# Zero rows for the low key parts of a differential attention, and another order of the first loads

## The chip, the cores and the metric

One core of a Trainium2 chip runs the whole program. The metric is the device time of one execution in microseconds (us). TensorE (PE in the rows, PEld for its weight loads) does the matmuls, VectorE (DVE) and ScalarE (ACT) the elementwise work, GpSimd (POOL) some small work, and SyncE (SP) issues most DMAs. The input and the weights lie in HBM and are read once.

## The reference

Two decoder layers over 256 tokens of width 1024, and a last norm. Of a layer, cut to what matters:

```python
h = _rms_norm(x, attn_norm)
proj = h @ w_in                       # q, k, v of A and B, latents of C, three gates
y_a = _diff_attention(aq, ak, av, lam, lam_init, slopes_a, diff_norm) @ w_branch_a
y_b = _dilated_attention(bq, bk, bv, slopes_b) @ w_branch_b
y_c = _mla(c_q, c_kv_pe, q_norm, w_uq, kv_norm, w_ukv, pos) @ w_branch_c
x = x + (g_a * y_a + g_b * y_b + g_c * y_c) @ w_out
h2 = _rms_norm(x, ffn_norm)
x = x + (silu(h2 @ w_ffn_gate) * (h2 @ w_ffn_up)) @ w_ffn_down

# in _diff_attention: 4 heads, each with 2 components c of 64 dimensions
s = einsum('bqhcd,bkhcd->bhcqk', q, k) * scale - slopes * dist     # causal
p = softmax(s); p = p[:, :, 0] - lam * p[:, :, 1]
```

## The kernel before

**Precision.** Every matmul works on pairs of fp32r tiles: a high part (ScalarE's copy that rounds, `hi_of`, L223) and the low part that is left (VectorE's difference, `lo_of`, L228 and L230). A product is the sum of three: high by high, high by low, low by high.

**Weights.** All weights are packed in the order of use into pieces of at most 128 x 1024 (`PLAN`). A piece is read into one of five `raw` buffers (`dma_piece`, L242, on SP's queue), split into one of five `whi` and `wlo` buffers (`split_piece`) and taken by TensorE (`take`). `split_piece` asks for the next DMA. The first eight pieces of a layer (128 x 672) make the latents of branch C, the next eight (128 x 1024) its differential queries and keys.

**Work in two streams.** `dense(l)` is a generator that yields after every piece; `run` and `attention` pull it by `pump(n)` between the small stages of attention (scores, softmax terms, transposes, values). The order of each engine's instructions then comes from a scheduler that reorders this program; its result is fixed when the program is built.

**The first 25 us.** `setup` issues, on SP: x transposed (`x0`, four tiles of f, 256 KB each, the first one in two halves), five weight pieces between them, then x once more in rows (`x_tm`, two tiles of 512 KB). `first_norm` splits `x0` into pairs and pumps one piece of the latent projection for each of its four tiles; then `squares` sums the squares of `x_tm` (L392), `norm_factors` makes the row factors r (L399, GpSimd's power in L373), `norm_diag` puts them on a diagonal (high and low half, L411 and L230) and `norm_rows` spreads them over all rows by two matmuls with ones (`ones_r`). The latents stay in two banks and two att buffers of PSUM until `latent_scaled` copies them out times r (L651, L654); `latent_transposed` transposes them (L692). The query and key tiles are copied out times the spread row factors (L513, L515).

**The stacked scores.** A head of branch A has two components of 64 dimensions, so one 128-row tile holds both. `stacked` makes for a query tile, per component c, a tile with the high part in the 64 rows of c and the low part in the other 64; for a key tile, per c, a tile with the high part in both halves, and one tile `low` that has the low parts of both components, each in its own 64 rows. One matmul of 128 rows then gives high by high plus low by high, and the third product needs 64 rows. `stacked_scores` (four heads, two components, two query blocks) issues

```python
self.mm(ps[:, 0:256], q[:, 128:256], kk, True, False)          # 128 rows
self.mm(ps[:, 0:256], q[rows, 128:256], low, False, True)      # rows: the 64 of c
```

and the same for the first query block with 128 columns, so a layer has 32 such matmuls, 16 of them with 64 rows.

**Room.** `fr` is a ring of 17 tiles of 128 x 1024, given out by halves or whole; `pt` a ring of 6 for the transposed probabilities; `row` one of 2 for the spread row factors.

Of the kernel before, what the change touches and what calls it, by code (L numbers as in the profile page):

```python
# [12 lines left out]
F32 = mybir.dt.float32  # L13
F32R = mybir.dt.float32r
# [17 lines left out]
SL = (slice(256, 384), slice(0, 256))  # L32
MASKED = 3.0e32
PIECE = 1024
N_PAIR = 17
N_F = 9
N_DENSE = 4
N_RAW = 5
# [145 lines left out]
class Build:  # L184
    def __init__(self, nc, tc, ctx, x, xt, w, gains, lam, fnorm, cst, out):
        self.nc, self.tc = nc, tc
        self.x_in, self.xt_in, self.w_in, self.gains_in = x, xt, w, gains
        self.lam_in, self.fnorm_in, self.cst_in, self.out = lam, fnorm, cst, out
        self.cp = cp = ctx.enter_context(tc.tile_pool(name="cp", bufs=1))
        pp = ctx.enter_context(tc.tile_pool(name="pp", bufs=1, space=PSUM))  # L190

        def ring(n, cols, dt, name, pool=cp):
            return Ring([pool.tile([128, cols], dt, name=f"{name}{i}") for i in range(n)])

        self.banks = ring(N_DENSE, 512, F32, "bank", pp)
        self.att = ring(8 - N_DENSE, 512, F32, "att", pp)
        self.fr = PairRing([cp.tile([128, 1024], F32R, name=f"fr{i}") for i in range(N_PAIR)])
        self.f = ring(N_F, 512, F32, "f")
        self.s = ring(5, 384, F32, "s")
        self.pt = ring(6, 384, F32R, "pt")  # L200
        self.small_tiles = ring(32, 4, F32, "small")
        self.row = ring(2, 256, F32, "row")
        self.raw = [cp.tile([128, PIECE], F32, name=f"raw{i}") for i in range(N_RAW)]
        self.whi = [cp.tile([128, PIECE], F32R, name=f"whi{i}") for i in range(N_PIECE)]
        self.wlo = [cp.tile([128, PIECE], F32R, name=f"wlo{i}") for i in range(N_PIECE)]
        self.taken = self.n_split = self.n_dma = self.woff = 0
# [82 lines left out]
    def setup(self):  # L289
        nc, cp = self.nc, self.cp  # L290
        self.gains = cp.tile([128, G_W], F32, name="gains")
        nc.scalar.dma_start(out=self.gains, in_=self.gains_in)
        self.x0 = [self.f.get() for _ in range(4)]
        x0 = [split_rows(t) for t in self.x0]
        self.x_tm = [cp.tile([128, D], F32, name=f"x_tm{b}") for b in range(2)]
        for p in range(4):
            if p == 0:
                nc.sync.dma_start(out=x0[0][:, 0], in_=self.x_in[:, 0, :])
                self.dma_piece()
                nc.sync.dma_start(out=x0[0][:, 1], in_=self.x_in[:, 1, :])  # L300
            else:
                nc.sync.dma_start(out=x0[p], in_=self.x_in[:, 2 * p:2 * p + 2, :])  # L302
                self.dma_piece()
        for _ in range(N_RAW - 4):
            self.dma_piece()
        for b in range(2):
            nc.sync.dma_start(out=self.x_tm[b], in_=self.xt_in[b])
        self.ones = cp.tile([128, 128], F32, name="ones")
        nc.vector.memset(self.ones, 1.0)
        self.ones_r = cp.tile([128, 128], F32R, name="ones_r")  # L310
        nc.vector.tensor_copy(self.ones_r, self.ones)
        warm = self.small()
        nc.scalar.activation(out=warm, in_=self.ones[:, 0:2], func=AF.Exp)
        bank = self.banks.get()
        for _ in range(WARM):
            self.mm(bank[:, 0:128], self.ones, self.ones, True, True)
        self.banks.put(bank)
        self.mhalf = cp.tile([128, 2], F32, name="mhalf")
        nc.gpsimd.memset(self.mhalf, -0.5)
        self.ident = cp.tile([128, 128], F32, name="ident")  # L320
        nc.sync.dma_start(out=self.ident, in_=self.cst_in[:, C_ID:C_ID + 128])
        self.vc = [cp.tile([128, 8, 2, 64], F32R, name=f"vc{b}") for b in range(2)]
        self.q_tm = cp.tile([128, 2, 8, 96], F32, name="q_tm")
        self.k_tm = cp.tile([128, 2, 8, 96], F32, name="k_tm")
        self.kpe = cp.tile([128, 2, 32], F32, name="kpe")

    def tables(self):
# [97 lines left out]
    def first_norm(self, pump):  # L425
        self.fresh_norm()
        for p in range(4):
            self.split_pair(p, split_rows(self.x0[p]), G_ATT)
            if p < AHEAD:
                self.split_piece()  # L430
            pump(1)
        self.f.put(*self.x0)
        self.ss = [self.small(), self.small()]
        for n in range(2):
            self.squares(n)
        self.norm_factors()
# [49 lines left out]
        self.split(*fields(kd[rows]), src)  # L486
        return kd

    def stacked(self, t, query):
        halves = (slice(0, 64), slice(64, 128))  # L490
        out = [self.fr.get() for _ in range(2)]
        for c in range(2):
            self.hi_of(out[c][halves[c]], t[halves[c]])
        if query:
            for c in range(2):
                self.lo_of(out[c][halves[1 - c]], t[halves[c]], out[c][halves[c]])
            return out
        low = self.fr.get()
        for c in range(2):
            self.hi_of(out[c][halves[1 - c]], t[halves[c]])  # L500
            self.lo_of(low[halves[c]], t[halves[c]], out[c][halves[c]])
        return out + [low]

    def qk_proj(self, q, k, scale, stacked):
        nc = self.nc
        for j in range(4):
# [8 lines left out]
                nc.vector.tensor_tensor(out=tv, in0=ps, in1=self.Rb, op=ALU.mult)  # L515
            self.banks.put(bank)
            if stacked:
                (q if j < 2 else k).append(self.stacked(t, j < 2))
            elif j < 2:
                hi, lo = self.fr.get(), self.fr.get()  # L520
                self.split(hi, lo, t)
                q.append((hi, lo))
            else:
                k.append(self.key_pair(tv))
# [212 lines left out]
    def stacked_scores(self, h, c):  # L737
        ps = self.att.get()
        cs = slice((h % 2) * 256, (h % 2) * 256 + 256)
        rows = slice(c * 64, c * 64 + 64)  # L740
        q, kk, low = self.qa[h // 2][c][:, cs], self.ka[h // 2][c][:, cs], self.ka[h // 2][2][rows, cs]
        self.mm(ps[:, 0:256], q[:, 128:256], kk, True, False)
        self.mm(ps[:, 0:256], q[rows, 128:256], low, False, True)
        self.mm(ps[:, 256:384], q[:, 0:128], kk[:, 0:128], False, False)
        self.mm(ps[:, 256:384], q[rows, 0:128], low[:, 0:128], False, True)
        return self.softmax_terms(ps, self.ta[h])

    def softmax_terms(self, ps, table, parts=False):
# [313 lines left out]
    def run(self):  # L1062
        self.n_norm = 0
        self.setup()
        for l in range(DEPTH):
            stream = self.dense(l)

            def pump(n):
                for _ in range(n):
                    next(stream)  # L1070
# [5 lines left out]
            else:  # L1076
                self.first_norm(pump)
            self.norm_diag()
            pump(2)
            self.norm_rows()  # L1080
            pump(2)
            self.latent_scaled()
            if l == 0:
                self.tables()
# [5 lines left out]
            pump(1)  # L1090
            self.latent_transposed(l, 2)
            self.latent_factors(l)
            pump(5)
            pump(5)
            pump(4)
            self.attention(l, pump)
            for _ in stream:
                pass
# [53 lines left out]
```

## Time and profile before

| | |
|---|---|
| median of 3 runs | 894.67 us (894.23 to 896.05) |
| profiled execution | 896.65 us, its span 894.8 us |
| TensorE, VectorE, ScalarE, GpSimd busy | 886.5, 591.9, 504.5, 66.4 us |
| mean granted TensorE clock | 0.997 |
| read from HBM | 154.03 MB, 173 GB/s over the span |

The span runs from the first to the last instruction, so 1.85 us of the profiled execution lie outside it. The execution that was profiled is 1.98 us longer than the median of the timed runs. A busy engine has an instruction in it; since matmuls overlap, the time that one of them costs is the distance from its start to the next one's start.

### The profile page before, as it was taken

The page shows a single profiled execution, that of the slowest core. Times are in us where ns is not written, and L with a number is a line of the kernel's source. Part 1 is how long each engine was busy: PE and PEld are TensorE (multiplying, and loading weights), DVE is VectorE, ACT ScalarE, POOL GpSimd, SP SyncE. Part 2 cuts the span into 40 slices and gives each one's busy share as a digit, 9 for nine tenths or more (in the row PEclk, how much of TensorE's full clock was granted, in tenths as well). Part 3 has the DMA queues.
Part 4 walks back from the last instruction along what each step waited for, and adds up shares of the span by engine and source line. Part 5 has one row for each costly group of instructions (what it writes and reads, how often), then busy time and mean ns, then how long its engine had stood idle before and what let it go on. Part 6 is the DMA issues. An engine that isn't in the chain of part 4 may idle for free.

```text
span 894.8 us, 12732 instructions
## 1 busy us (share of the span) xinstructions
PE 886.5 (99%) x4710; PEld 763.9 (85%) x4710; DVE 591.9 (66%) x990; ACT 504.5 (56%) x852; POOL 66.4 (7%) x91
## 2 busy tenths in 40 slices
PE   9999999999999999999999999999999999999997
PEld 8988988888888888888899799888888888888886
DVE  6967978756665666555467778787655666556444
ACT  7875766654554444444376767766444554444332
POOL 1830220000000000000011303000000000000000
PEclk9999999999999999999999999999999999999999
DMA  9745344456556666666465454444565566655541
GB/s 336 256 145 188 119 142 145 139 170 196 180 172 196 189 188 183 183 179 191 142 210 176 139 169 138 142 144 161 166 203 173 165 203 197 193 187 185 188 142 48
DMA packets 45423, 155.92 MB, mean 174 GB/s; under 512 B 5168, under 2 KB 6192, under 8 KB 45360
## 3 DMA queue, kind: packets, MB, share of 16 engines
q1 hardware_dynamic: 44928, 154.55, 54.4%
q8 instruction: 37, 0.61, 0.3%
q10 hardware_dynamic: 432, 0.55, 0.2%
q14 instruction: 26, 0.21, 0.1%
HBM read 154.03 MB, written 1.05 MB: 173 GB/s over the span
## 4 chain that ended last, share of the span: by engine, by line
PE 97%; DMA 1%; issue 1%; SPq 0%; ACT 0%; DVE 0%; POOLq 0%; POOL 0%
PE bank L210 85%; PE att L210 7%; PE att L443 2%; DMA x_tm<-xt 1%; PE att L718 1%; PE att L767 0%; PE att L769 0%; PE att L768 0%; ACT f L392 0%; SPq L242 0%; PE att L692 0%; PE att L851 0%; DVE x_tm L1043 0%; SPq L302 0%; ACT x_tm L1058 0%
## 5 line engine op out<-in xcount | busy, mean ns | idle before, releaser
L210 PE MATMUL bank<-whi,fr 128*128 128x512 f32 (+1 forms) x2032 | 632.6, 387 | 1.1 <-ACT whi L223 1.1
L228 DVE TENSOR_TENSOR wlo<-raw,whi 128x1024 fp32r<-128x1024 f32 (+2 forms) x294 | 353.3, 1203 | 250.3 <-ACT whi L223 249.1
L223 ACT ACTIVATE whi<-raw 128x1024 fp32r<-128x1024 f32 (+2 forms) x294 | 305.0, 1040 | 309.8 <-PE bank L210 255.3
L210 PEld LDWEIGHTS bank<-whi,fr 128*128 128x128 f32 x2032 | 380.4, 188 | 73.9 <-ACT whi L223 1.6
L210 PE MATMUL bank<-wlo,fr 128*128 128x512 f32 (+1 forms) x1016 | 390.6, 386 | 0.0
L210 PEld LDWEIGHTS bank<-wlo,fr 128*128 128x128 f32 x1016 | 191.3, 188 | 36.3 <-DVE wlo L228 0.9
L210 PE MATMUL bank<-fr,whi 128*128 128x256 f32 x512 | 95.3, 285 | 0.0
L210 PEld LDWEIGHTS bank<-fr,whi 128*128 128x128 f32 x512 | 80.1, 191 | 0.2
L210 PE MATMUL bank<-fr,wlo 128*128 128x256 f32 x256 | 73.0, 285 | 0.0
L210 PEld LDWEIGHTS bank<-fr,wlo 128*128 128x128 f32 x256 | 49.0, 191 | 0.0
L373 POOL TENSOR_TENSOR r<-small,mhalf 128x2 f32<-128x2 f32 x4 | 2.8, 706 | 480.0 <-DVE small L399 480.0
L759 ACT ACTIVATE s<-s,small 128x256 f32<-128x256 f32 (+1 forms) x80 | 35.7, 450 | 3.5 <-DVE small L757 3.2
L210 PE MATMUL att<-fr,fr 96*128 96x256 f32 (+5 forms) x184 | 36.5, 301 | 0.0
L210 PEld LDWEIGHTS att<-fr,fr 96*128 96x128 f32 (+2 forms) x184 | 28.3, 188 | 7.0 <-issue 1.4
L223 ACT ACTIVATE fr<-att 128x512 fp32r<-128x512 f32 (+2 forms) x54 | 28.4, 558 | 6.7 <-PE att L210 4.0
L373 POOL TENSOR_TENSOR small<-small,mhalf 128x2 f32<-128x2 f32 (+1 forms) x12 | 10.1, 844 | 294.1 <-DVE small L1047 178.5
L210 PE MATMUL att<-whi,fr 128*128 128x288 f32 (+1 forms) x108 | 29.8, 289 | 0.0
L228 DVE TENSOR_TENSOR fr<-att,fr 128x512 fp32r<-128x512 f32 (+2 forms) x46 | 28.2, 636 | 0.9 <-ACT fr L223 0.6
L223 ACT ACTIVATE fr<-f 64x512 fp32r<-64x512 f32 (+2 forms) x40 | 23.3, 582 | 5.0 <-DVE f L513 2.7
L972 ACT ACTIVATE f<-bank,rh 128x512 f32<-128x512 f32 (+1 forms) x24 | 15.6, 654 | 12.2 <-PE bank L210 12.2
L614 ACT ACTIVATE f<-bank,rh 128x512 f32<-128x512 f32 x24 | 16.3, 689 | 8.7 <-PE bank L210 8.5
L228 DVE TENSOR_TENSOR fr<-f,fr 64x512 fp32r<-64x512 f32 (+2 forms) x32 | 20.2, 631 | 0.4
(130 smaller groups left out, 615.4 us busy)
## 6 DMA issues: line engine op xcount, KB each, us to landing
raw<-w SPq DMA_DIRECT2D x272, 512.0 KB, 3.6
raw<-w SPq DMA_DIRECT2D x16, 336.0 KB, 3.1
raw<-w SPq DMA_DIRECT2D x6, 384.0 KB, 3.6
x_tm<-xt SPq DMA_DIRECT2D x2, 512.0 KB, 8.0
f<-x SPq DMA_DIRECT2D x3, 256.0 KB, 5.3
f<-fnorm SPq DMA_DIRECT2D x2, 256.0 KB, 4.2
out<-x_tm ACTq DMA_DIRECT2D x2, 256.0 KB, 2.2
f<-x SPq DMA_DIRECT2D x2, 128.0 KB, 2.9
```

The costliest lines, as they stand in the source:

```text
L210: self.nc.tensor.matmul(out, lhsT, rhs, start=start, stop=stop, skip_group_check=True)
L223: self.nc.scalar.activation(out=hi, in_=src, func=AF.Copy, scale=scale)
L228: self.nc.vector.tensor_tensor(out=lo, in0=src, in1=h, op=ALU.subtract)
L373: self.nc.gpsimd.tensor_tensor(out=out, in0=v, in1=self.mhalf[:, 0:v.shape[1]], op=ALU.pow)
L443: self.nc.tensor.transpose(ps[:, c, b * 128:b * 128 + 128], src[b][:, c0 + c * 128:c0 + c * 128 + 128], self.ident)
L614: nc.scalar.activation(out=t[b], in_=bank[b], func=AF.Tanh, scale=self.rh[:, b:b + 1])
L718: nc.tensor.transpose(ps[0:96, c, b * 128:b * 128 + 128], src[:, b, 2 * p + c, :], self.ident)
L759: nc.scalar.activation(out=s[:, SL[b]], in_=s[:, SL[b]], func=AF.Exp, bias=mn[:, b:b + 1], scale=-1.0, accum_out=z[:, b:b + 1])
L972: nc.scalar.activation(out=a, in_=g, func=AF.Tanh, scale=self.rh[:, b:b + 1])
```

## The change

- The low parts of the differential keys move from halves of the `fr` ring into four tiles of their own (`low`, one per key tile and component). Each has the low part of component c in the 64 rows of c and zeros in the other 64, which GpSimd writes once in `setup`. The matmul with the low part then takes all 128 rows of the query tile; its number and its columns stay the same.
- To make room, `fr` has 16 tiles (the low parts leave it), `pt` 5 and `row` 1.
- On SP the second weight piece is asked for ahead of the second tile of x, and so on, one piece before each tile; `x_tm` is no longer issued in `setup` but after the third and the fourth `pump` of `first_norm`.
- In layer 0 five pieces more are pumped ahead of the squares, and the pumps behind `norm_diag` and `norm_rows` and one later one fall away: 25 in all, as before. In layer 1 the numbers stay.

```diff
-N_PAIR = 17
+N_PAIR = 16
...
-        self.pt = ring(6, 384, F32R, "pt")
+        self.pt = ring(5, 384, F32R, "pt")
...
-        self.row = ring(2, 256, F32, "row")
+        self.row = ring(1, 256, F32, "row")
...
-        for p in range(4):
-            if p == 0:
-                nc.sync.dma_start(out=x0[0][:, 0], in_=self.x_in[:, 0, :])
-                self.dma_piece()
-                nc.sync.dma_start(out=x0[0][:, 1], in_=self.x_in[:, 1, :])
-            else:
-                nc.sync.dma_start(out=x0[p], in_=self.x_in[:, 2 * p:2 * p + 2, :])
-                self.dma_piece()
-        for _ in range(N_RAW - 4):
+        nc.sync.dma_start(out=x0[0][:, 0], in_=self.x_in[:, 0, :])
+        self.dma_piece()
+        nc.sync.dma_start(out=x0[0][:, 1], in_=self.x_in[:, 1, :])
+        self.dma_piece()
+        for p in range(1, 4):
+            nc.sync.dma_start(out=x0[p], in_=self.x_in[:, 2 * p:2 * p + 2, :])
             self.dma_piece()
-        for b in range(2):
-            nc.sync.dma_start(out=self.x_tm[b], in_=self.xt_in[b])
...
+        self.low = [[cp.tile([128, 512], F32R, name=f"low{j}_{c}") for c in range(2)] for j in range(2)]
+        for low in self.low:
+            for c in range(2):
+                nc.gpsimd.memset(low[c][64 - c * 64:128 - c * 64].bitcast(F32), 0.0)
...
             pump(1)
+            if p >= 2:
+                self.nc.sync.dma_start(out=self.x_tm[p - 2], in_=self.xt_in[p - 2])
         self.f.put(*self.x0)
+        pump(5)
...
-    def stacked(self, t, query):
+    def stacked(self, t, query, j):
...
-        low = self.fr.get()
         for c in range(2):
             self.hi_of(out[c][halves[1 - c]], t[halves[c]])
-            self.lo_of(low[halves[c]], t[halves[c]], out[c][halves[c]])
-        return out + [low]
+            self.lo_of(self.low[j - 2][c][halves[c]], t[halves[c]], out[c][halves[c]])
+        return out
...
-        rows = slice(c * 64, c * 64 + 64)
-        q, kk, low = self.qa[h // 2][c][:, cs], self.ka[h // 2][c][:, cs], self.ka[h // 2][2][rows, cs]
+        q, kk, low = self.qa[h // 2][c][:, cs], self.ka[h // 2][c][:, cs], self.low[h // 2][c][:, cs]
         self.mm(ps[:, 0:256], q[:, 128:256], kk, True, False)
-        self.mm(ps[:, 0:256], q[rows, 128:256], low, False, True)
+        self.mm(ps[:, 0:256], q[:, 128:256], low, False, True)
         self.mm(ps[:, 256:384], q[:, 0:128], kk[:, 0:128], False, False)
-        self.mm(ps[:, 256:384], q[rows, 0:128], low[:, 0:128], False, True)
+        self.mm(ps[:, 256:384], q[:, 0:128], low[:, 0:128], False, True)
...
             self.norm_diag()
-            pump(2)
+            if l:
+                pump(2)
             self.norm_rows()
-            pump(2)
+            if l:
+                pump(2)
             self.latent_scaled()
...
-            pump(5)
-            pump(5)
-            pump(4)
+            pump(14 if l else 13)
```

What the scheduler makes of it, at the places of which the prediction speaks. SP's queue, from its fourth DMA on, behind two halves of x and the first piece (f are the tiles of x0, raw the weight pieces), before:

```order
L302 DMA f_87<-x 128x512
L242 DMA raw_141<-w 128x672
L302 DMA f_88<-x 128x512
L242 DMA raw_142<-w 128x672
L302 DMA f_89<-x 128x512
L242 DMA raw_143<-w 128x672
L242 DMA raw_144<-w 128x672
L307 DMA x_tm_157<-xt 128x1024
L307 DMA x_tm_158<-xt 128x1024
L321 DMA ident<-cst 128x128
L242 DMA raw_140<-w 128x672
L242 DMA raw_141<-w 128x672
```

and with the change:

```order
L242 DMA raw_138<-w 128x672
L301 DMA f_86<-x 128x512
L242 DMA raw_139<-w 128x672
L301 DMA f_87<-x 128x512
L242 DMA raw_140<-w 128x672
L301 DMA f_88<-x 128x512
L242 DMA raw_141<-w 128x672
L316 DMA ident<-cst 128x128
L242 DMA raw_137<-w 128x672
L242 DMA raw_138<-w 128x672
L432 DMA x_tm_154<-xt 128x1024
L432 DMA x_tm_155<-xt 128x1024
```

Pieces two to five each stand one tile of x earlier, and pieces six and seven now stand ahead of both tiles of x_tm.

TensorE's queue where the latent projection (bank_62 and bank_63, att_65 and att_66) ends and the first query tile (bank_64) begins, before (the two matmuls with ones_r stand further up, in the projection; the first transpose of a latent, out of f, comes 24 matmuls of the query tile later):

```order
L210 MATMUL bank_63<-whi_147,fr_72 128x384
L210 MATMUL att_66<-whi_147,fr_72 128x288
L210 MATMUL bank_64<-fr_69,whi_148 128x256 x2
L210 MATMUL bank_64<-fr_69,wlo_153 128x256
L210 MATMUL bank_64<-fr_69,whi_148 128x256 x2
```

and with the change (fr_73 is the diagonal, f_93 and f_85 are scaled latents):

```order
L210 MATMUL bank_63<-whi_144,fr_72 128x384
L210 MATMUL att_66<-whi_144,fr_72 128x288
L210 MATMUL att_67<-fr_73,ones_r 128x256
L210 MATMUL bank_64<-fr_69,whi_145 128x256 x2
L210 MATMUL att_67<-fr_73,ones_r 128x256
L693 MATMUL att_68<-ident,f_93 128x128
L693 MATMUL att_65<-ident,f_85 128x128
L210 MATMUL bank_64<-fr_69,wlo_150 128x256
L210 MATMUL bank_64<-fr_69,whi_145 128x256 x2
```

Both matmuls with ones and two transposes now stand among the first matmuls of the query tile.

TensorE's queue at the first scores of layer 0 (fr_78 and fr_79 hold keys, fr_74 the queries; every second row is the low part), before:

```order
L210 MATMUL att_66<-fr_78,fr_74 128x256
L210 MATMUL att_66<-fr_79,fr_74 128x256
L210 MATMUL att_66<-fr_78,fr_74 128x128
L210 MATMUL att_66<-fr_79,fr_74 128x128
L210 MATMUL att_68<-fr_78,fr_74 128x256
```

and with the change:

```order
L210 MATMUL att_66<-fr_78,fr_73 128x256
L210 MATMUL att_66<-low_0_189,fr_73 128x256
L210 MATMUL att_66<-fr_78,fr_73 128x128
L210 MATMUL att_66<-low_0_189,fr_73 128x128
L210 MATMUL att_68<-fr_78,fr_73 128x256
```

The same matmuls in the same order, the low parts out of their own tiles. Behind the third head's scores the new order has the transposes of the rotated queries (q_tm), which stood after the value projection.

## Rows read from the trace of the kernel before

**Rows 1.** The page: TensorE's and others' busy time; ScalarE's weight splits, busy and idle.

```profile
PE 886.5 (99%) x4710; PEld 763.9 (85%) x4710; DVE 591.9 (66%) x990; ACT 504.5 (56%) x852; POOL 66.4 (7%) x91
L223 ACT ACTIVATE whi<-raw 128x1024 fp32r<-128x1024 f32 (+2 forms) x294 | 305.0, 1040 | 309.8 <-PE bank L210 255.3
```

**Rows 2.** What TensorE waited for: us in total, times, longest.

```profile
PE bank L210 <- ACT whi L223: 1.1, 2, 0.9
```

**Rows 3.** Timeline of TensorE, scores of layer 0 and one follower: start, us.

```profile
53.08 2.86 PE L210 MATMUL att<-fr,fr 128*128 128x256 f32 x10
55.87 0.76 PE L210 MATMUL bank<-whi,fr 128*128 128x512 f32 x1
...
61.70 1.35 PE L210 MATMUL att<-fr,fr 128*128 128x128 f32 x5
...
64.44 2.60 PE L210 MATMUL att<-fr,fr 64*128 64x128 f32 x9
...
87.50 2.23 PE L210 MATMUL att<-fr,fr 128*128 128x256 f32 x8
```

**Rows 4.** Timeline of TensorE, scores of layer 1 and one follower.

```profile
494.75 2.86 PE L210 MATMUL att<-fr,fr 128*128 128x256 f32 x10
497.54 0.50 PE L210 MATMUL bank<-whi,fr 128*128 128x512 f32 x1
...
500.38 1.61 PE L210 MATMUL att<-fr,fr 128*128 128x128 f32 x6
...
504.79 2.23 PE L210 MATMUL att<-fr,fr 128*128 128x256 f32 x8
...
527.42 2.23 PE L210 MATMUL att<-fr,fr 128*128 128x256 f32 x8
```

**Rows 5.** Timeline of TensorE, full-height matmuls: 24 alike, then five values matmuls.

```profile
43.83 0.28 PE L210 MATMUL bank<-fr,wlo 128*128 128x256 f32 x1
...
46.71 0.28 PE L210 MATMUL bank<-fr,wlo 128*128 128x256 f32 x1
...
95.39 0.69 PE L210 MATMUL att<-fr,pt 128*128 128x128 f32 x5
95.92 0.60 PE L718 MATMUL att<-ident,q_tm 128*96 128x128 f32 x4
```

**Rows 6.** Busy time by stretch: PE, PEld, DVE, ACT, POOL, clock, DMA share, GB/s.

```profile
10.00:15.00 5.00, 5.00 (x34) 5.00 (x34) 3.42 (x6) 4.14 (x9) 0.00 (x0) 1.00 1.04 413
48.00:68.00 20.00, 20.00 (x83) 15.64 (x82) 12.63 (x40) 16.02 (x39) 7.10 (x8) 0.91 0.44 132
55.50:59.50 4.00, 4.00 (x11) 3.07 (x11) 3.91 (x11) 2.10 (x9) 3.92 (x4) 0.57 0.54 145
494.50:498.50 4.00, 4.00 (x17) 2.75 (x16) 3.36 (x8) 4.00 (x10) 3.92 (x6) 1.00 0.35 121
```

**Rows 7.** The page: a full-height weight load, busy and mean ns.

```profile
L210 PEld LDWEIGHTS bank<-fr,whi 128*128 128x128 f32 x512 | 80.1, 191 | 0.2
```

**Rows 8.** Timelines of ScalarE, TensorE, GpSimd and VectorE in the first 25 us.

```profile
4.37 0.76 ACT L223 ACTIVATE whi<-raw 128x672 fp32r<-128x672 f32 x1 [0.31 <-DMA raw<-w]
...
7.70 0.76 ACT L223 ACTIVATE whi<-raw 128x672 fp32r<-128x672 f32 x1 [0.75 <-DMA raw<-w]
...
8.52 0.44 PE L210 MATMUL bank<-whi,fr 128*128 128x384 f32 x1 [0.94 <-ACT whi L223]
...
13.20 0.63 ACT L392 ACTIVATE f<-x_tm 128x512 f32<-128x512 f32 x1 [0.51 <-DMA x_tm<-xt]
...
16.21 0.70 POOL L373 TENSOR_TENSOR r<-small,mhalf 128x2 f32<-128x2 f32 x1 [15.39 <-DVE small L399]
...
16.57 0.44 PE L210 MATMUL bank<-whi,fr 128*128 128x384 f32 x1 [0.15 <-ACT whi L223]
...
18.62 0.61 DVE L230 SCALAR_TENSOR_TENSOR fr<-ident,r,fr 128x128 fp32r<-128x128 f32 x2
...
23.10 0.58 ACT L651 ACTIVATE f<-bank,r 128x384 f32<-128x384 f32 x1
```

More of the change, by code (lines that the diff above doesn't have):

```diff
@@ L517, in qk_proj @@
             if stacked:
-                (q if j < 2 else k).append(self.stacked(t, j < 2))
+                (q if j < 2 else k).append(self.stacked(t, j < 2, j))
             elif j < 2:
```

## The prediction

> **What bounds the kernel now.** I read the page's engine line first: TensorE is busy for 886.5 of 894.8 us, VectorE for 592 and ScalarE for 505 [rows 1]. Then the waits of TensorE: the longest total on any releaser is 1.1 us [rows 2], while ScalarE's weight splits alone spend 255 us waiting for TensorE to give a weight buffer back [rows 1]. So TensorE sets the end nearly everywhere, and a change pays here if it takes time out of TensorE's own queue, or out of the first 20 us, where it still waits for data. "Busy" doesn't mean "at its peak", though: how long its matmuls take from start to start has to be read from the timeline.
>
> Read that way, one kind of work stands out. The stacked scores of layer 0 come as 10, 5, 9 and 8 matmuls in 2.86, 1.35, 2.60 and 2.23 us [rows 3], those of layer 1 as 10, 6, 8 and 8 in 2.86, 1.61, 2.23 and 2.23 us [rows 4]. Of the first ten, the next matmul starts 55.87 - 53.08 = 2.79 us after the first: 0.28 us each. Half of them have 64 rows, and they alternate with matmuls of 128 rows. Where only full-height matmuls follow each other, 24 of 256 columns take 46.71 - 43.83 = 2.88 us, 0.120 each, and a run of five with 128 and 256 columns mixed takes 95.92 - 95.39 = 0.53 us, 0.106 each [rows 5]. All matmuls of the scores are therefore drawn out to more than twice their pitch, the 128-row ones too: each change between 64 and 128 rows empties the engine.
>
> The second loss is in the clock. From 55.5 to 59.5 us the granted clock averages 0.57 [rows 6]; it is the lower of the two levels (1.2 GHz of 2.4) for 3.4 us in that stretch, and what ran just before it fell was the 2.8 us of drawn-out scores. In layer 1 the same ten matmuls are followed by no fall: 1.00 from 494.5 to 498.5 us [rows 6].
>
> **Term 1, the scores.** 64 matmuls take 9.04 + 8.93 = 17.97 us by their durations; the last matmul of each of the eight groups overlaps its follower by 0.07 us (2.86 against 2.79), so they hold the queue for 17.4 us. After the change all 64 are full-height, same number, same columns. At 0.106 us each they take 6.8, at 0.120 us 7.7; half have 128 columns and half 256, so I take 0.112 and 7.2 us: **10.2 us saved** (9.7 to 10.6). The matmul behind each group also has to wait for the last drain; bounded by nothing below and by one more drawn-out step (0.28 - 0.11 = 0.17 us, eight times 1.4 us) above, I add 0.5. Term 1 is **10.7 us, 9.7 to 12.0**. The zeros cost nothing per matmul, since time goes by columns in these rows and not by rows.
>
> One rule of the Trainium skill speaks against this. TensorE: Matmul & The Clock Gate, Part 3, says that a weight load overlaps a matmul in flight only when the row group differs. Full-height matmuls all use every row group, so by that rule the padded scores would put load and matmul end to end and the term would be nothing or a loss. In this trace a full-height load takes 191 ns [rows 7] and full-height matmuls still start 120 ns apart [rows 5], so here the loads are hidden, and the sum goes by the row.
>
> **Term 2, the clock.** 0.43 of 4.00 us is **1.7 us**. If the stretch before it is filled with matmuls at 0.11 us, I expect no fall, but a fall after 494.75 us did not happen with the same work, so when it comes is partly chance: 0 to 1.7.
>
> **Term 3, the front.** Today the second weight piece lands at 7.70 us, TensorE is idle for 0.94 us until 8.52, and more while it waits for that piece's low part; at 16.57 it waits again, because the sixth piece lands, and is split, behind the 1 MB of x_tm and its squares [rows 8]. The change puts the second piece ahead of 256 KB of x. Between the first piece (4.37) and 7.70 us 720 KB pass: 128 KB of x, then the 336 KB, then 256 KB of x. By share the second piece lands at 4.37 + 3.33 x 464/720 = 6.5 us, its high part (0.76 us) is ready at 7.3, and TensorE, done with the first piece at 7.58, doesn't wait for it; the low part (0.9 us) is ready as its fifth matmul comes up. That takes out about 1.2 us, and with pieces six and seven now ahead of x_tm another 0.4: the latent projection ends some 1.6 us earlier, near 21 us.
>
> But x_tm now lands later by two pieces, 688 KB at 413 GB/s [rows 6], 1.7 us. The row factors and the low half of the diagonal follow it; that ends at 18.62 + 0.61 = 19.2 us today [rows 8] and at about 20.9 then, just when its matmul is wanted: no wait, and no slack. And the order has two transposes of the scaled latents after only two matmuls of the first query tile. Their inputs are evictions by ScalarE that can start only when the projection has ended, about 0.58 us each [rows 8]: 1.1 us, of which 0.5 is covered by the two ones matmuls and the two query matmuls. TensorE waits 0.6 to 0.8 us there. Everything behind it on TensorE's queue waits too. Term 3 is 1.6 - 0.8 = **0.8 us** (-0.5 if x_tm lands another 1.3 us later, 1.6 if the evictions are hidden).
>
> **Term 4, what is given back.** ScalarE is busy for 16.0 of the 20 us from 48 to 68 [rows 6]. Term 1 (three of the four groups, about 4.1 us) and term 2 shorten that stretch to 14.2 us, less than ScalarE's own work in it. The excess of 1.8 us is mostly weight splitting for pieces used later, which ScalarE does ahead of need and can move behind 68 us; nothing to 2.5 us for both layers, and I take **0.8**, since the new order also asks for the rotated queries (q_tm) right behind the third head's scores, ahead of the value projection, and GpSimd has to have rotated them by then.
>
> The four memsets of the zero halves are GpSimd's while it has nothing else (its first work on data is the row factors at 16.21 us [rows 8]), and the smaller rings (16 pairs, 5 transposed tiles, 1 row tile) are reused two units later than they are read: nothing, unless a reader is late.
>
> **Sum.** 10.7 + 1.7 + 0.8 - 0.8 = 12.4 us. The profiled execution took 896.65 us (span 894.8 and 1.85 around it), the median of the runs is 894.67; against the profile the sum gives 884.2, against the median **882.3 us**. Bounds: 12.0 + 1.7 + 1.6 = 15.3 gives 879.4; 9.7 + 1.7 - 0.5 - 2.5 = 8.4 gives 886.3.
>
> **Rivals.**
> - *The fall of the clock stays or comes elsewhere.* For it: nothing in the rows says what exactly set it off, and the new wait near 21 us is a place. Against it: layer 1. Price 1.7 us: 884.0. Chance 0.16.
> - *ScalarE or VectorE becomes the bound around the scores.* For it: 16.0 of 14.2 us. Against it: the 255 us for which weight splits wait for TensorE. Price, the 1.8 us of layer 0 and as much in layer 1, on top of the 0.8: 885.1. Chance 0.10.
> - *The padding doesn't speed the scores up* (loads end to end, as in the sentence on the skill above, or a drain that has another cause than the rows). Then the 64 matmuls stay at 0.27 us, the fall of the clock stays, and only term 3 is left: 893.9. Rows 5 speak against it. Chance 0.03.
> - *Slower:* x_tm is late. Until the row factors exist, the ones matmuls stand in TensorE's queue ahead of all query matmuls, and nothing passes them; each us by which x_tm lands later than 1.7 us behind today costs one us. It decides from 12.4 us on: with 14 us it would be 896.3. Against it: at 413 GB/s that would take 5 MB more in front of it, and only 688 KB are. Chance 0.03.
>
> **How the numbers follow.** The sum as it stands has 0.68: 882.3, own range 879.4 to 886.3. The first two rivals lie inside or at the upper end of it, so 879.5 to 887.0 us leaves out the last two rivals and about 0.1 of the tails. A measurement of this kernel can tell about 0.2% (1.8 us) from no change, so faster means below 892.9: 0.94 (the sum and the first two rivals). Same: 0.03, the third rival. Slower: 0.03, the fourth.
>
> **What would show it.** Right: the ten first scores of a layer take about 1.1 us, and no row of 64 rows is left; the granted clock is 1.00 from 50 to 60 us; TensorE's wait at 8.52 is gone or below 0.3 us, with a new one of 0.6 to 0.8 us between 20 and 23 us for a latent's eviction; the first scores start about 1 us earlier than 53.08. Wrong: padded scores still near 0.28 us each (then the rows were not the cause); a wait of several us in front of the ones matmuls; waits of TensorE for weight splits or q_tm from 50 to 70 us that add to more than 2.5 us; a lower clock at a new place.

## The result and the profile after

The changed kernel takes **883.88 us** (median of four runs, 883.18 to 884.57), beside 895.36 us (894.23 to 896.52) of the kernel before in the same job: ratio 0.9872, 95% interval 0.9855 to 0.9889. Forecast were 882.3 us in 879.5 to 887.0, and faster with 0.94. A second set of four runs of the same kernel (experiment 10) gave 883.72 (883.48 to 883.79). The profiled execution took 883.18 us with a span of 881.4; that of before had 894.8, so the two traces differ by 13.4 us, more than the medians do. The clock explains most of that (below).

The page of the changed kernel: busy time by engine, and the shares of its chain of waits:

```profile
PE 873.6 (99%) x4710; PEld 759.5 (86%) x4710; DVE 591.1 (67%) x990; ACT 502.2 (57%) x852; POOL 71.4 (8%) x95
...
PE 97%; POOL 1%; issue 1%; DVE 0%; ACT 0%; POOLq 0%
```

VectorE and ScalarE do the work that they did [rows 1], and GpSimd has 5.0 us more, its four fills with zeros (0.52 us each) among them. TensorE's busy time has shrunk by 12.9 us, with as many instructions. What TensorE waited for, in the changed kernel (us in total, times, longest):

```profile
PE bank L210 <- DVE ones L304: 1.0, 1, 1.0
PE att L719 <- POOL q_tm L605: 0.5, 1, 0.5
```

The wait of 1.0 us is the program's first microsecond. The one for weight splits [rows 2] is gone, and a new one stands there, for the rotated queries. The timeline of TensorE (start us, us, what) at the first scores of layer 0:

```profile
51.62 0.28 PE L210 MATMUL att<-fr,fr 128*128 128x256 f32 x1
51.74 0.28 PE L210 MATMUL att<-low,fr 128*128 128x256 f32 x1
51.85 0.23 PE L210 MATMUL att<-fr,fr 128*128 128x128 f32 x1
51.92 0.28 PE L210 MATMUL att<-low,fr 128*128 128x128 f32 x1
...
52.77 0.40 PE L210 MATMUL bank<-whi,fr 128*128 128x512 f32 x1
```

The first of them start 0.12, 0.11 and 0.07 us apart (0.06 to 0.17 within the ten, 0.115 on average), and what follows the ten starts 52.77 - 51.62 = 1.15 us after the first, where it took 2.79 [rows 3]. The single lengths of 0.28 us are still there, but they overlap: read starts, not lengths. Over all eight groups, from the first start to that of the follower, the 64 matmuls hold the queue for 17.3 us before and 7.04 after.

The first place where the old order idled, in the changed kernel: ScalarE's split of the second piece, and TensorE's first matmul with it:

```profile
6.95 0.77 ACT L223 ACTIVATE whi<-raw 128x672 fp32r<-128x672 f32 x1 [1.18 <-DMA raw<-w]
...
7.77 0.45 PE L210 MATMUL bank<-whi,fr 128*128 128x384 f32 x1
```

Before, that split started at 7.70, and TensorE resumed at 8.52 [rows 8]. Where the latent projection ends, ScalarE's evictions and TensorE's transposes (L693):

```profile
20.54 0.58 ACT L652 ACTIVATE f<-bank,r 128x384 f32<-128x384 f32 x1 [0.40 <-PE bank L210]
21.02 0.49 ACT L655 ACTIVATE f<-att,r 128x288 f32<-128x288 f32 x1
...
20.89 0.29 PE L210 MATMUL att<-whi,fr 128*128 128x288 f32 x1
21.02 0.28 PE L210 MATMUL att<-fr,ones_r 128*128 128x256 f32 x1
...
21.50 0.39 PE L693 MATMUL att<-ident,f 128*128 128x128 f32 x2
21.65 0.36 PE L210 MATMUL bank<-fr,wlo 128*128 128x256 f32 x1
```

The first eviction starts 0.35 us before the projection's last matmul does, and the transposes go in without a wait. Behind the third head's scores, TensorE's transposes of the rotated queries, and GpSimd's last rotation:

```profile
59.78 0.28 PE L719 MATMUL att<-ident,q_tm 128*96 128x128 f32 x1
60.62 0.54 PE L719 MATMUL att<-ident,q_tm 128*96 128x128 f32 x3 [0.55 <-POOL q_tm L605]
...
59.83 0.73 POOL L605 TENSOR_TENSOR q_tm<-f,f 128x256 f32<-128x256 f32 x1
```

The first transpose reads the half that is ready; the second starts 0.84 us later instead of 0.11: 0.73 us given back. And the stretches of [rows 6], around the scores, in the changed kernel:

```profile
48.00:68.00 20.00, 19.45 (x106) 17.12 (x105) 17.81 (x52) 19.91 (x50) 7.54 (x8) 1.00 0.54 171
50.00:60.00 10.00, 10.00 (x60) 8.92 (x58) 8.19 (x22) 9.94 (x23) 6.98 (x8) 1.00 0.62 191
```

The clock is 1.00 throughout; ScalarE is busy for 19.91 of 20 us (16.02 before), and TensorE waits only for GpSimd there.

### The profile page after: what moved, and what is told of

It is laid out like the page before. It is cut to its first block, busy times and chain, and to the rows that moved or that the text cites. A ratio compares the mean times of both kernels' runs of the same rounds, so it can differ in the third digit from the quotient of the medians.

```text
span 881.4 us, 12736 instructions
## 1 busy us (share of the span) xinstructions
PE 873.6 (99%) x4710; PEld 759.5 (86%) x4710; DVE 591.1 (67%) x990; ACT 502.2 (57%) x852; POOL 71.4 (8%) x95
## 4 chain that ended last, share of the span: by engine, by line
PE 97%; POOL 1%; issue 1%; DVE 0%; ACT 0%; POOLq 0%
PE bank L210 87%; PE att L210 6%; PE att L445 2%; PE att L719 1%; PE att L767 0%; PE att L768 0%; PE att L769 0%; POOL f L602 0%; PE att L693 0%; PE att L851 0%; POOL f L604 0%; POOL f L603 0%; POOL q_tm L605 0%; DVE x_tm L1043 0%; ACT x_tm L1058 0%
## 5 line engine op out<-in xcount | busy, mean ns | idle before, releaser
L210 PE MATMUL att<-fr,fr 96*128 96x256 f32 (+3 forms) x152 | 26.0, 277 | 0.0
L210 PEld LDWEIGHTS att<-fr,fr 96*128 96x128 f32 (+1 forms) x152 | 22.7, 190 | 0.6
L972 ACT ACTIVATE f<-bank,rh 128x512 f32<-128x512 f32 (+1 forms) x24 | 15.6, 654 | 12.2 <-PE bank L210 12.2
L210 PEld LDWEIGHTS att<-whi,fr 128*128 128x128 f32 x108 | 20.4, 191 | 0.1
```

The lines of the kernel that those rows point to most:

```text
L210: self.nc.tensor.matmul(out, lhsT, rhs, start=start, stop=stop, skip_group_check=True)
L972: nc.scalar.activation(out=a, in_=g, func=AF.Tanh, scale=self.rh[:, b:b + 1])
```

## The experiments

The theory: the rows cost the time, 10.7 us of it, because each change between 64 and 128 rows empties TensorE; the front is a small matter of its own; the two together give something back where the rotated queries are late. The rivals: the ring sizes or the order of the matmuls did it; the columns or the loads, not the changes of height, set the price; the front did more.

**1. The padding alone** (front and pumps of before):

```diff
-        low = self.fr.get()
...
-            self.lo_of(low[halves[c]], t[halves[c]], out[c][halves[c]])
+            self.lo_of(self.low[j - 2][c][halves[c]], t[halves[c]], out[c][halves[c]])
...
-        self.mm(ps[:, 0:256], q[rows, 128:256], low, False, True)
+        self.mm(ps[:, 0:256], q[:, 128:256], low, False, True)
```

> The kernel before with the zero-padded low tiles and the smaller rings, and the first loads, pumps and squares as they were. If the scores' changes of height are what cost (my theory): the 64 stacked matmuls hold TensorE for 7.0 us instead of 17.3, the clock stays full around them, the front keeps its waits: 12 us less than before, 1.5 us more than the changed kernel, about 885. If the front is most of the gain (rival): 892 or more.

Measured: 884.02 us (883.87 to 884.03), ratio 0.9869 (0.9856 to 0.9882). Its scores hold 7.04 us, and there is no wait for q_tm. The padding is nearly the whole result: this kernel is 0.14 us slower than the changed one, where 1.5 were expected, so the front adds far less to the padding than forecast.

**2. The front alone** (requests and pumps of the change, scores of before):

```diff
+        nc.sync.dma_start(out=x0[0][:, 1], in_=self.x_in[:, 1, :])
+        self.dma_piece()
+        for p in range(1, 4):
+            nc.sync.dma_start(out=x0[p], in_=self.x_in[:, 2 * p:2 * p + 2, :])
...
+            if p >= 2:
+                self.nc.sync.dma_start(out=self.x_tm[p - 2], in_=self.xt_in[p - 2])
```

> The kernel before with the new order of the first loads and pumps only; the scores alternate between 128 and 64 rows as before. My theory: first scores about 1.5 us earlier than 53.08, groups of scores as long as before (2.79 us for ten), about 1.5 us less than before, within what the measurement can tell; a fall of the clock behind the scores may or may not come. Rival (the front is most of the gain): 885 or less.

Measured: 893.83 us (892.98 to 898.64, ten runs), ratio 0.9992 (0.9978 to 1.0006): by its interval no difference. In its trace the scores start at 51.89 instead of 53.08 us, 1.2 earlier (0.8 to 1.0 earlier than in experiments 1 and 8, which have the old front and start at 52.85 and 52.66). The six executions without a fall of the clock have a median of 893.55, where those of before without one average 894.8 (median 894.7). So the front is worth some 1.2 us by itself, under what the interval can tell.

**3. The same kernel with low parts of 64 rows** (TensorE's queue is that of the change, instruction for instruction):

```diff
-        q, kk, low = self.qa[h // 2][c][:, cs], self.ka[h // 2][c][:, cs], self.low[h // 2][c][:, cs]
+        rows = slice(c * 64, c * 64 + 64)
+        q, kk, low = self.qa[h // 2][c][:, cs], self.ka[h // 2][c][:, cs], self.low[h // 2][c][rows, cs]
...
-        self.mm(ps[:, 0:256], q[:, 128:256], low, False, True)
+        self.mm(ps[:, 0:256], q[rows, 128:256], low, False, True)
```

> The changed kernel, same order of TensorE's queue word for word, but the matmul with the low part takes the 64 rows of its component again, out of the same zero-padded tiles. My theory (changes of height): all 10.3 us of the scores come back, 17.3 us for the 64 matmuls, 0.5 us more behind the groups, and perhaps a fall of the clock (1.7 us): 11 to 12.5 us slower than the changed kernel. Rival (it is the tiles of their own, or the new order, that makes the scores fast): within 1 us of the changed kernel.

Measured: 894.02 us (893.54 to 895.78), ratio 0.9984 (0.9975 to 0.9993). The timeline of TensorE in this kernel, at the same place as above:

```profile
51.85 0.28 PE L210 MATMUL att<-fr,fr 128*128 128x256 f32 x1
52.06 0.38 PE L210 MATMUL att<-low,fr 64*128 64x256 f32 x1
52.37 0.33 PE L210 MATMUL att<-fr,fr 128*128 128x128 f32 x1
52.63 0.32 PE L210 MATMUL att<-low,fr 64*128 64x128 f32 x1
52.88 0.39 PE L210 MATMUL att<-fr,fr 128*128 128x256 f32 x1
```

Steps of 0.21, 0.31, 0.26 and 0.25 us: nothing but the height of every second matmul differs, and the 64 hold 17.3 us again. Zero rows take 10.1 us out of the median (11 to 12.5 were expected). The rule in TensorE: Matmul & The Clock Gate, Part 3, of the Trainium skill (in its list of what overlaps, a load overlaps only where the row group differs, though the text above that list also allows the background weight buffer) would have left the padded scores no gain over these; the trace disagrees, with steps of 0.11 us on average in the padded scores.

The weight loads (PEld) show where the time goes. In the changed kernel, the load for the matmul that starts at 51.74:

```profile
51.62 0.19 PEld L210 LDWEIGHTS att<-low,fr 128*128 128x128 f32 x1
```

and in this one, the loads for the second and the third matmul of the list above:

```profile
52.06 0.18 PEld L210 LDWEIGHTS att<-low,fr 64*128 64x128 f32 x1 [0.19 <-issue]
52.37 0.19 PEld L210 LDWEIGHTS att<-fr,fr 128*128 128x128 f32 x1
```

With one height the load starts with the matmul before its own, here 0.12 us ahead, and is hidden behind it (0.05 to 0.12 us ahead at all 56 steps inside the eight groups). Where the height changes, it starts together with its own matmul, at all 56 steps. My estimate from these rows: a step of 0.31 us is a load that is no longer hidden (0.18) and the 0.12 that the same matmul takes in the padded kernel. Whether the load waits because the engine has to be empty first, as the prediction has it, or for another reason, the trace doesn't tell.

This run also shows the give-back: here TensorE comes to the rotated queries some 4 us later (64.1 against 59.8) and doesn't wait, so the 0.73 us is missing from the difference: 17.33 - 7.04 = 10.29, some 0.4 at the followers, less 0.73, is 10.0.

**4. The 64-row matmuls in pairs** (two of 128 rows, then two of 64, instead of alternating):

```diff
-        q, kk, low = self.qa[h // 2][c][:, cs], self.ka[h // 2][c][:, cs], self.low[h // 2][c][:, cs]
+        rows = slice(c * 64, c * 64 + 64)
+        q, kk, low = self.qa[h // 2][c][:, cs], self.ka[h // 2][c][:, cs], self.low[h // 2][c][rows, cs]
...
-        self.mm(ps[:, 0:256], q[:, 128:256], low, False, True)
         self.mm(ps[:, 256:384], q[:, 0:128], kk[:, 0:128], False, False)
-        self.mm(ps[:, 256:384], q[:, 0:128], low[:, 0:128], False, True)
+        self.mm(ps[:, 0:256], q[rows, 128:256], low, False, True)
+        self.mm(ps[:, 256:384], q[rows, 0:128], low[:, 0:128], False, True)
```

> As the kernel with 64 rows in the changed order, but each component's four matmuls stand as 128, 128, 64, 64 rows: half as many changes of height, as many matmuls of 64 rows. If each change of height costs (my theory): two of four steps are at the full-height pitch, the 64 matmuls take about (17.3 + 7.0) / 2 = 12.2 us, 5 us less than with alternating heights. If each 64-row matmul costs, whatever its neighbours (rival): three of four steps stay drawn out, about 14.7 us, 2.6 us less.

Measured: 887.88 us (887.88 to 889.27), ratio 0.9916 (0.9903 to 0.993). The 64 matmuls hold 11.13 us, below the 12.2 expected and far from the rival's 14.7. Half the changes, and 4.09 us above the padded scores instead of 10.29: 0.13 us for each of 32 changes, 0.16 for each of 64. The columns and the number of 64-row matmuls are the same, so it is the change of height that costs. At the second matmul of each pair the load is ahead of its matmul again, by 0.11 to 0.12 us. "Mode switching requires drain" is the sentence for it in the Trainium skill (TensorEngine Tiling (Array Packing), Key Properties); it gives no price, and the traces agree that there is one.

**8. The smaller rings alone:**

```diff
-        self.pt = ring(6, 384, F32R, "pt")
+        self.pt = ring(5, 384, F32R, "pt")
...
-        self.row = ring(2, 256, F32, "row")
+        self.row = ring(1, 256, F32, "row")
```

> The kernel before with pt of 5 and row of 1, nothing else; scores with 64 rows. My theory: the smaller rings cost nothing; time as before within 0.1%, and some executions with a fall of the clock behind the first scores, as in the kernel before. Rival (smaller rings cost part of the gain): 1 us or more slower, with waits of ScalarE for the transposed tiles.

Measured: 895.35 us (894.14 to 896.54), ratio 0.9998 (0.9989 to 1.0007). They cost nothing, as forecast. Its trace shows something else as well. TensorE's timeline behind the third head's scores, and a stretch of 3.4 us there (columns as in [rows 6], the clock third from the end):

```profile
62.37 2.60 PE L210 MATMUL att<-fr,fr 64*128 64x128 f32 x9
64.90 0.50 PE L210 MATMUL bank<-whi,fr 128*128 128x512 f32 x1
65.24 0.46 PE L210 MATMUL bank<-wlo,fr 128*128 128x512 f32 x1
65.50 1.05 PE L210 MATMUL bank<-whi,fr 128*128 128x512 f32 x2
...
65.43:68.84 3.41, 3.41 (x9) 2.64 (x8) 3.37 (x12) 2.15 (x11) 0.00 (x0) 0.50 0.29 68
```

The clock falls to 1.2 GHz here too, for 3.4 us, but behind another group of scores than in the trace of before [rows 6].

**5, 6, 7: where the front's gain goes.** Three edits of the changed kernel. Five: every pair's rotated queries asked for one head later. Six: x_tm asked for in `setup` again, behind the early pieces. Seven: the pieces asked for late, as before, with x_tm late.

```diff
-LAG_T, LAG_V, LAG_O, LAG_X = 3, 4, 6, 2
+LAG_T, LAG_V, LAG_O, LAG_X = 3, 4, 6, 1
```

> The changed kernel with the transposes of the rotated queries and keys one unit later in the program (LAG_X 1 for 2), so that they no longer stand right behind the third head's scores. If GpSimd's rotation is what TensorE waited for at 60 us (my theory): that wait is gone, 0.7 us less than the changed kernel, about 883.2. Rival: the transposes wait or push something else later, and the time stays within 0.5 us or rises.

Measured: 884.31 us (884.01 to 885.43). The wait for q_tm is gone from its trace, and from the first scores to layer 1's first it is 0.23 us shorter than the changed kernel's (434.82 against 435.05), but between the 2,900th and the 3,200th matmul, in layer 1's attention, it loses 0.74. It isn't faster, where 0.7 us less were expected. (The profiled execution is its slowest, 885.43.)

```diff
+        for b in range(2):
+            nc.sync.dma_start(out=self.x_tm[b], in_=self.xt_in[b])
...
-            if p >= 2:
-                self.nc.sync.dma_start(out=self.x_tm[p - 2], in_=self.xt_in[p - 2])
```

> The changed kernel with x_tm asked for in the setup again, behind the first five pieces: pieces six and seven land behind its 1 MB. My theory: the second piece still comes early, TensorE waits again near 16 us for the sixth piece (about 0.4 us in all), and the first scores start about 0.4 us later than 51.62; the time within 0.5 us of the changed kernel. Rival (all of the front's gain is in x_tm's place): first scores near 53.

Measured: 884.9 us (884.7 to 885.38). TensorE's timeline in this kernel, at the sixth piece:

```profile
16.80 0.44 PE L210 MATMUL bank<-whi,fr 128*128 128x384 f32 x1 [1.15 <-ACT whi L223]
```

The wait is 1.15 us where 0.4 was expected. The first scores start at 51.72, but that says little: the scheduler put them nine matmuls earlier in this kernel, and the 149th matmul of the queue starts at 26.50 us, against 24.80 in the changed kernel.

```diff
-        self.dma_piece()
-        for p in range(1, 4):
-            nc.sync.dma_start(out=x0[p], in_=self.x_in[:, 2 * p:2 * p + 2, :])
+            else:
+                nc.sync.dma_start(out=x0[p], in_=self.x_in[:, 2 * p:2 * p + 2, :])
+                self.dma_piece()
+        for _ in range(N_RAW - 4):
             self.dma_piece()
```

> The changed kernel with the second to fifth piece behind the tiles of x as before; x_tm stays late. My theory: TensorE's wait of 0.9 us at 8.5 us is back, the first scores start about 1.1 us later than 51.62; since GpSimd's rotation is then ready in time, most of the 0.7 us lost at 60 us is not lost, and the time is within 0.7 us of the changed kernel. Rival (the second piece is not what TensorE waits for): first scores at 51.6.

Measured: 884.81 us (884.67 to 885.47). TensorE's timeline in this one:

```profile
8.12 0.44 PE L210 MATMUL bank<-whi,fr 128*128 128x384 f32 x1 [0.17 <-ACT whi L223]
...
22.70 0.39 PE L210 MATMUL bank<-fr,wlo 128*128 128x256 f32 x1 [0.67 <-DVE wlo L228]
...
62.23 0.53 PE L722 MATMUL att<-ident,q_tm 128*96 128x128 f32 x3 [0.55 <-POOL q_tm L608]
```

The wait at the second piece is 0.17 us, not the 0.9 expected, and there is more behind the projection. The first scores start at 52.92, 1.3 later than 51.62, about as expected. But the wait for q_tm is still there, as long as in the changed kernel, where the theory had it gone: GpSimd's last rotation ends 1.6 us later too. So that wait comes from where the new order puts the transposes, with padded scores in front of them (experiment 3, with the same queue and slow scores, has none), and not from an early front.

Both expectations of the time (within 0.5 and 0.7 us of the changed kernel) were missed, by 1.0 and 0.9. Both are slower than the changed kernel, and neither is better than the padding with the old front. Two more experiments take the half that was left, and the kernel itself once more on the same chip.

**11. The padding, and of the front only the early weight pieces** (two to five, each one tile of x earlier; x_tm and pumps as before, and TensorE's queue that of experiment 1):

```diff
-            if p == 0:
-                nc.sync.dma_start(out=x0[0][:, 0], in_=self.x_in[:, 0, :])
-                self.dma_piece()
-                nc.sync.dma_start(out=x0[0][:, 1], in_=self.x_in[:, 1, :])
...
+        nc.sync.dma_start(out=x0[0][:, 1], in_=self.x_in[:, 1, :])
+        self.dma_piece()
```

> The padding with the front of before, except that the second weight piece is asked for ahead of the first tiles of x (x_tm and the order of the pieces' matmuls as before). If the idle 0.94 us ahead of the second piece's matmuls is all that this request takes out and nothing behind gives it back, 1.0 us less than the padding alone (884.02): 883.0, and as good as the whole new front. If what comes earlier is waited for again at the attention's start, as in the changed kernel, 883.9 to 884.2.

Measured: 884.47 us (884.22 to 884.55), outside both expectations (883.0, and 883.9 to 884.2) and no better than the padding alone. TensorE's timeline, at the sixth piece again, and ScalarE's in front of it:

```profile
16.91 0.44 PE L210 MATMUL bank<-whi,fr 128*128 128x384 f32 x1 [0.77 <-ACT whi L223]
...
15.50 0.61 ACT L393 ACTIVATE f<-x_tm 128x512 f32<-128x512 f32 x1
16.02 0.19 ACT L393 ACTIVATION_READ_ACCUMULATOR f<-x_tm 128x1 f32 x1
16.11 1.48 ACT L223 ACTIVATE whi<-raw 128x672 fp32r<-128x672 f32 x2
```

There is no wait at the second piece any more, but the sixth is split behind the squares of x_tm, whenever TensorE gets there: what was won at 8 us is waited out at 16.9 (the same matmul starts at 16.36 in experiment 1). Here the projection ends when x_tm's squares let it.

**10. The changed kernel again**, unedited, beside 9 and 11:

> The changed kernel itself, beside the other two on the same chip, for its median over more runs: 883.9, between 883.2 and 884.6 as before. If its front, whose transfers are asked for in a tight row, varies by a microsecond from execution to execution (first scores at 51.6 us in one trace, at 53.6 us in another kernel with the same order of matmuls up to there), the runs spread over 1 us or more; if the front's gain of 1.2 us in the first trace was typical, they lie at 883.2.

Measured: 883.72 us (883.48 to 883.79); the spread is 0.3 us here, not the 1 us expected of a variable front. First scores at 51.81, wait for q_tm 0.56.

**9. The first pair's rotated queries of layer 0 one head later, the rest as in the change:**

```diff
-            run(s + LAG_X, 0)
+            if l or s != 2:
+                run(s + LAG_X, 0)
+            if not l and s == 3:
+                run(4, 0)
```

> The changed kernel, with the transposes of the first pair's rotated queries (q_tm) in layer 0 asked for one head later, behind the fourth head's scores; the order of the matmuls ahead of that and all of layer 1's requests stay as they are. If the wait of 0.55 us for GpSimd's q_tm near 60 us (0.73 us from start to start) is what the new front's gain is lost to, this kernel has no such wait and takes 0.5 to 0.7 us less than the changed kernel run beside it: 883.2 to 883.4. If the loss only moves on (ScalarE and VectorE, busy for nearly all of 48 to 68 us, then hold up the softmax rows instead), the two agree within 0.3 us, as the kernel that asked for every pair one head later (884.31) suggests.

Measured: 883.33 us (883.22 to 883.42): 0.39 less than experiment 10, beside which it ran, and the two ranges don't overlap. By its median it is the fastest kernel of this study, by 0.04%; one of the first four executions of the changed kernel, in another job, took 883.18. TensorE's timeline at the place of the old wait:

```profile
60.56 0.28 PE L210 MATMUL att<-low,fr 128*128 128x128 f32 x1
60.67 0.33 PE L210 MATMUL att<-fr,fr 128*128 128x256 f32 x1
...
61.02 0.28 PE L210 MATMUL att<-low,fr 128*128 128x128 f32 x1
61.13 0.45 PE L210 MATMUL bank<-whi,fr 128*128 128x512 f32 x1
```

The fourth head's scores stand where TensorE waited. From the first scores to the end of the span this trace is 0.44 us shorter than that of 10 (881.5 - 52.05 against 881.7 - 51.81). It saves less than the 0.73 at stake, because part of it comes back behind: between the rival and the theory, nearer the theory.

## Why the prediction was right, point by point

**Term 1, the scores: right.** 10.7 forecast; 10.3 measured in the 64 matmuls, and about 0.4 in the followers (in layer 1, 238 instead of 334 ns behind the first group and 283 instead of 335 behind the second). Experiment 3 puts it on the rows, and 4 on the changes between heights. The prediction's words for the cause, a change that empties the engine, say more than the traces do: they show that at a change the weight load is no longer hidden. The rival "padding doesn't speed the scores up" falls with them.

**Term 2, the clock: right in the trace, wrongly charged to the median.** No fall is left, but I took 1.7 us off a median that had not paid it. Of 42 executions of the kernel before that ran beside the experiments, 24 show a mean granted clock of 0.997 or less and average 896.4 us; the other 18 average 894.8. The 1.6 between them is the price of one such stretch. The 894.67 from which I subtracted lies with the 18; the profiled execution, 896.65, with the 24. Against the latter my sum gave 884.2, and the changed kernel's profile took 883.18; the 882.3 was too low by 1.6, which is this term. It belonged to half of the executions, some 0.9 on an average one. The rival "the fall stays" has by chance the right time, 884.0, and the wrong reason: the changed kernel's trace shows no fall.

**Term 3, the front: too large up to the scores, and wrong in both parts.** The forecast was 1.6 us gained and 0.8 waited at the transposes. The first scores start 1.3 to 1.5 us earlier in the changed kernel's two traces than in that of before (51.62 and 51.81 against 53.08). But with the same number of matmuls ahead, three traces with the old front have 53.08, 52.85 and 52.66, and of seven with the new one six have 51.62 to 52.16 and one 53.55 (experiment 5): about 1 us is typical. So the 0.8 that the sum took is near it by luck, from a gain that was too large and a wait that didn't come. The wait didn't come: I took the evictions to start when the projection had ended, but it ends bank by bank, and the first bank is evicted from 20.54 us on. And the gain is not 1.2 of the second piece plus 0.4 of the sixth: TensorE's first matmul with the second piece starts 0.75 us earlier (7.77 against 8.52), the one with the sixth 1.06 earlier (15.51 against 16.57), and the first scores 1.46. Neither half alone made the padded kernel faster (6 and 7 keep the new pumps, 11 has the old ones; the pumps alone were not tried): without the late x_tm the second piece's gain is waited out at the sixth (6 and 11), and without the early pieces TensorE waits at 22.7 us for a low part (7). x_tm was not late: the low half of the diagonal ends at 20.33 us, before the projection does.

**Term 4, given back: right, at one of the two places.** 0.8 forecast, 0.73 measured, all of it at the rotated queries; experiments 3 and 9 show it from both sides, and 7 that it doesn't need an early front. ScalarE, at 19.91 of 20 us, held up nothing: weight splits were ahead, as the row in favour of this said [rows 1], so the rival that made ScalarE the bound falls. (Its 885.1 is 2.8 us above the sum, which is 3.6 in place of the 0.8; added on top of the 0.8, as its words have it, it would be 885.9.)

**What stays open.** Padding alone saves 10.8 us, front alone 1.2 (both against executions without a fall), and together they save 10.9 to 11.1. Of the 0.9 to 1.1 that is missing, experiment 9 gets 0.4 back. Behind layer 1's first scores nothing is lost: from there to the end of the span the changed kernel's two traces take 394.73 us, and that of the padding alone 394.72. Between the first scores of the two layers the changed kernel takes 0.5 to 0.65 us more than the padding alone (435.05 and 435.16 against 434.51), and experiment 9 0.2 more (434.72). Where the rest lies I can't show: traces of one order of matmuls already differ by more at the first scores (51.62 in the changed kernel, 53.55 in experiment 5, whose queue is the same up to there, and where the early pieces took 6.4 instead of 5.4 us to land).

## What to carry to other kernels

Where matmuls of 64 and of 128 rows alternate, look at the steps from start to start: filling the short ones with zeros up to the full height cost nothing per matmul here and saved 0.16 us a change, and where zeros can't be had, grouping them by height may do: in pairs it saved more than half of it. Before subtracting a mishap that a profile shows (a fall of the clock, a late transfer), ask whether the median has it. Look at the weight loads too: a load that starts together with its own matmul is not hidden. An early transfer is worth only what the next thing behind it on the same path doesn't wait for anyway: follow the path to the one that ends last, here x_tm's squares in front of the sixth piece.

## What the runs showed of the hardware

In every trace with both heights, the load for a matmul of the other height starts within 0.002 us of its own matmul (56 of 56 changes inside the groups of before, 2, 3 and 8, 24 of 24 of experiment 4); with one height it starts 0.05 to 0.12 us ahead of it, and in the padded scores the matmuls follow each other every 0.11 us on average though a load takes 0.19.

The fall of the clock comes and goes by execution. Kernels with alternating heights (before, 2, 3 and 8) have a mean clock of 0.997 or less in 36 of 74 executions, those with padded or paired scores (the change, 1, 4 to 7, 9 to 11) in 0 of 36. In both traces that caught it, it lasts 3.4 us and begins within 0.6 us of the end of a group of alternating scores, the first group in one and the third in the other, while TensorE is busy without a gap; what decides whether it comes was not found. The paired 64-row matmuls, with half the changes, showed none in their four executions.
